# A list schedule that knows TensorE's tilings, and the recurrence's outputs issued in two groups

## The chip, the cores and the metric

The kernel runs on one core of a Trainium2 chip. The metric is device time in microseconds (us) of one execution; the time before is the median of three runs. A core has five engines that run side by side, each through its own list of instructions in order: TensorE (PE in the profile) multiplies matrices, with the loading of the stationary operand shown apart as PEld; VectorE (DVE), ScalarE (ACT) and GpSimd (POOL) work elementwise; SyncE (SP) issues DMAs. An instruction that needs another engine's result waits on a semaphore.

## The reference, cut to what matters

The program is two blocks, one after the other, on 512 tokens of width 1024, all in float32. The first block has two layers (feed-forward, a mixer, feed-forward). The second has two layers, each with three mixers side by side: full attention, neighbourhood attention, and a recurrence with a matrix state for each of six heads, run forwards and backwards, first over a context of 256 tokens and then over the 512 tokens. The change touches the code of this recurrence:

```python
def _rwkv7_step(S, inp):
    r, w, k, v, kk, b = inp
    sa = jnp.einsum('bhvk,bhk->bhv', S, kk)
    S = S * w[:, :, None, :] - sa[..., None] * b[:, :, None, :] + v[..., None] * k[:, :, None, :]
    return S, jnp.einsum('bhvk,bhk->bhv', S, r)
...
    S_f, y_f = lax.scan(_rwkv7_step, S0_f, (r, decay[:, :, 0], kd[:, :, 0], v, kk, bd[:, :, 0]))
    S_b, y_b = lax.scan(_rwkv7_step, S0_b, (r, decay[:, :, 1], kd[:, :, 1], v, kk, bd[:, :, 1]),
                        reverse=True)
```

## The kernel before, in words

**How it is written.** The code does not issue instructions. It records them as `Op` objects, in the order of the program text (with `par` weaving parts that are independent), and `schedule` puts all of them into one order before any is issued; `emit` then issues them, which is why nearly every row of the profile has one line, L568. So a change of the planner's prices can move any instruction of the kernel.

**The planner.** `Op._cost` gives each instruction a price in microseconds. `simulate` is a list scheduler over the five engines: an instruction may start when all that it depends on has ended, plus `lag` (a `LATENCY` by the engine that produced it, nothing from TensorE to TensorE), and when there is a free slot for each new tile. On each engine the ready instruction with the best `key` is taken. `schedule` calls it six times, in turn backwards in time (which gives the keys) and forwards (which gives the order). On TensorE there is one more rule: a ready matmul of the same kind as the last is preferred, if its key is no more than `STAY` = 2.0 us behind the best one. Before the change there are two kinds, `small` (price under 0.1 us) and not small.

**Prices on TensorE.** Before the change, a float32r matmul (one pass over the array) costs 1/2.4 ns a column plus 2 ns, a float32 one four times as much a column, and times 0.58 where its stationary operand has 17 to 64 columns. Large products are made of three float32r matmuls of up to 512 columns (`mm3`); small ones are float32, and the profile shows each float32 matmul as two records.

**Tilings.** A matmul uses a part of the 128 x 128 array: its stationary operand's rows and columns, each rounded up to 32, 64 or 128. This text calls that pair the tiling (128x128, 128x64, 64x64, 64x32, ...), and a place in TensorE's order where the tiling differs from the matmul before a switch. Matmuls of one tiling may stand at different places of the array.

**The recurrence** (`rwkv_d`) takes 32 tokens a step, four steps a block of 128. A step is: six matmuls zeta S of tiling 64x32, two subtractions on VectorE that give the rows of u in the tile `UV`, six matmuls of tiling 64x64 that add to the state, an addition on VectorE that gives the next S. After each fourth step the block's outputs are made: 24 matmuls rho S with the four old states (tiling 64x32, `KR` times `old`), and 12 matmuls Q [u; v] (tiling 128x64, `EQ` times `UV`), into two PSUM tiles `py`, one for each parity of the head. They are recorded as four rho S, two Q [u; v], six times over. There are 20 such blocks in the program (four in the first layer's context, eight in each layer's tokens), so 480 matmuls rho S and 240 Q [u; v]; in the profile rho S and zeta S are `ps<-S,t`, and Q [u; v] is `ps<-uv,t` with 128*64.

Of the kernel before, what the change touches and what calls it, by code (L numbers as in the profile page):

```python
# [12 lines left out]
F32R = mybir.dt.float32r  # L13
# [3 lines left out]
P = 128  # L17
# [246 lines left out]

SLOTS = dict(t=70, raw=4, ps=8, big=3, uv=1, S=14, tmp=2, s8=48, s32=16, s64=4)
ENGINES = ("tensor", "vector", "scalar", "gpsimd", "sync")
LATENCY = dict(tensor=0.2, vector=0.14, scalar=0.15, gpsimd=0.15, sync=3.0)
AHEAD = dict(sync=25.0)
AHEAD_ALL = 80.0
BACK = 500  # L270
# [83 lines left out]
class Op:  # L354
    def __init__(self, eng, method, a, k):
        self.eng, self.method, self.a, self.k = eng, method, a, k
        named = [(f"#{i}", x) for i, x in enumerate(a)] + list(k.items())
        refs = [(q in ("#0", "out", "accum_out"), x) for q, x in named if isinstance(x, Ref)]
        self.writes = [x for w, x in refs if w]
        self.reads = [x for w, x in refs if not w]  # L360
        self.cost = self._cost()
        self.small = self.cost < 0.1 and eng == "tensor"

    def _cost(self):

        n = max([x.cols() for x in self.writes + self.reads] or [1])
        ps = any(x.base.kind == "ps" for x in self.reads)
        if self.eng == "tensor":
            n = self.writes[0].cols()
            if self.method == "transpose":  # L370
                return 0.84e-3 * n
            l = self.k["lhsT"]
            f = 1 / 2.4 if l.base.dt == F32R else 4 / 2.4
            half = 0.58 if 16 < l.cols() <= 64 else 1.0
            return 0.002 + 1e-3 * max(n, 64) * f * half
        if self.eng == "vector":
            if self.method == "reciprocal":
                return 0.065 + 6.25e-3 * n
            fast = not ps and self.method in ("tensor_scalar", "tensor_copy", "memset")
            return 0.07 + n * (0.52e-3 if fast else 1.04e-3) + 0.06 * any(isinstance(self.k.get(q), Ref) for q in ("scalar", "scalar1"))  # L380
        if self.eng == "scalar":
            return (0.051 if ps else 0.094) + 0.833e-3 * n + 0.09 * ("accum_out" in self.k)
        if self.eng == "gpsimd":
            return 0.28 + 0.166 * n if self.k.get("op") == ALU.pow else 0.03 + (0.84e-3 if self.method == "memset" else 2.25e-3) * n
        return 0.05 + 1.65e-3 * n
# [55 lines left out]
def simulate(ops, before, after, key, lag, ahead):  # L441


    n = len(ops)
    left = [len(d) for d in before]
    uses, slot, start = {}, {}, [0.0] * n
    for op in ops:
        for t in op.slotted:
            uses[id(t)] = uses.get(id(t), 0) + 1
    empty = {k: [(0.0, i) for i in range(m)] for k, m in SLOTS.items()}  # L450
    ready, free = [0.0] * n, dict.fromkeys(ENGINES, 0.0)
    wait = {e: [] for e in ENGINES}
    can = {e: [] for e in ENGINES}
    small = False
    first, head, done, order = sorted(range(n), key=key.__getitem__), 0, [False] * n, []
    for i in range(n):
        if not left[i]:
            heapq.heappush(wait[ops[i].eng], (0.0, i))

    def room(i, tight):  # L460

        need = {}
        for t in ops[i].slotted:
            if id(t) not in slot:
                need[t.kind] = need.get(t.kind, 0) + 1
        at = 0.0
        for k, m in need.items():
            if len(empty[k]) - m < (0 if tight or i == first[head] else RESERVE.get(k, 0)):
                return None
            at = max(at, heapq.nsmallest(m, empty[k])[-1][0])  # L470
        return at

    def best(tight):
        out = None
        for e in ENGINES:
            limit = key[first[head]] + ahead(e)
            while wait[e] and wait[e][0][0] <= free[e]:
                i = heapq.heappop(wait[e])[1]
                heapq.heappush(can[e], (key[i], i))
            for src, time in ((can[e], lambda x: free[e]), (wait[e], lambda x: x[0])):  # L480
                pick = None
                for x in sorted(src):
                    i = x[1]
                    if key[i] > limit or pick and key[i] > pick[1] + STAY:
                        if src is can[e]:
                            break
                        continue
                    if pick and ops[i].small != small:
                        continue
                    at = room(i, tight)  # L490
                    if at is not None:
                        pick = (max(at, time(x)), key[i], i, e, src, x)
                        if e != "tensor" or src is not can[e] or ops[i].small == small:
                            break
                if pick:
                    break
            if pick and (out is None or pick[:2] < out[:2]):
                out = pick
        return out

    while len(order) < n:
        while done[first[head]]:
            head += 1
        pick = best(False) or best(True)
        if pick is None:
            return None
        at, _, i, e, src, x = pick
        if e == "tensor":
            small = ops[i].small
        src.remove(x)  # L510
        heapq.heapify(src)
        end = free[e] = at + ops[i].cost
        start[i], done[i] = at, True
        order.append(i)
        for t in ops[i].slotted:
            if id(t) not in slot:
                slot[id(t)] = heapq.heappop(empty[t.kind])[1]
            uses[id(t)] -= 1
            if not uses[id(t)]:
                heapq.heappush(empty[t.kind], (end + 0.1, slot[id(t)]))  # L520
        for j in after[i]:
            ready[j] = max(ready[j], end + lag(i, j))
            left[j] -= 1
            if not left[j]:
                heapq.heappush(wait[ops[j].eng], (ready[j], j))
    return order, slot, [start[i] + ops[i].cost for i in range(n)]


def schedule(ops):

    n = len(ops)
    for op in ops:
        op.slotted = [t for t in op.tiles() if t.kind in SLOTS]
    before = dependences(ops)
    after = [[] for _ in range(n)]
    for i, d in enumerate(before):
        for j in d:
            after[j].append(i)  # L540
    lag = lambda i, j: 0.0 if ops[i].eng == ops[j].eng == "tensor" else LATENCY[ops[i].eng]
    key, far, out = [-float(i) for i in range(n)], BACK, None
    for _ in range(ROUNDS):
        back = simulate(ops, after, before, key, lambda i, j: lag(j, i), lambda e: far)
        ahead = back and simulate(ops, before, after, [-x for x in back[2]], lag, lambda e: AHEAD.get(e, AHEAD_ALL))
        if not ahead:
            break
        out, key, far = ahead, [-x for x in ahead[2]], AGAIN
    return [ops[i] for i in out[0]], out[1]
# [22 lines left out]
class Prog:  # L572
# [47 lines left out]
    def row(self):  # L620
        return self.t2((4, T))
# [1211 lines left out]
    def rwkv_d(self, d, q, r, S):  # L1833


        n, nb, need_y = d["n"], d["nb"], d["need_y"]
        UV = d["UV"]
# [3 lines left out]
        both = [(j, par) for j in range(3) for par in range(2)]  # L1841
        for step in range(4 * nb):
            g = 4 * nb - 1 - step if r else step
            b, c = g // 4, g % 4
            row = lambda c, par: 64 * (c % 2 ^ par)
            if step % 4 == 0:
                old = {}
# [3 lines left out]
            for j, par in both:  # L1851
                o, ro = 64 * par, row(c, par)
# [7 lines left out]
            for j, par in both:  # L1860
                o, ro = 64 * par, row(c, par)
# [3 lines left out]
            self.tt(S, pn, keep, ALU.add)  # L1865
            if not need_y or step % 4 < 3:
                continue
            py = [self.ps((P, 3, 64)) for _ in range(2)]
            for a in range(2):
                for j in range(3):  # L1870
                    for i, par in ((0, 0), (0, 1), (1, 0), (1, 1)):
                        o, cc = 64 * par, 2 * a + (i ^ par)
                        s = P * (b % 2) + 32 * cc
                        self.mm(py[par][32 * cc:32 * cc + 32, j], q["KR"][j][b // 2][o:o + 64, 1, s:s + 32],
                                old[cc][o:o + 64, j], stop=False)
                    for par in range(2):
                        self.mm(py[par][64 * a:64 * a + 64, j], q["EQ"][2 * j + par][:, 2 * b + a], UV[:, b, a, 2 * j + par],
                                start=False)
            for par in range(2):
                y = d["y"][b][:, par::2]  # L1880
                if first:
# [207 lines left out]
```

## Time and profile before

| | |
|---|---|
| time before, median of three runs | 3327.55 us (3325.96 to 3327.77) |
| the profiled execution: its own time | 3327.22 us |
| its span, first to last instruction | 3325.4 us |
| TensorE busy | 3217.1 us (97% of the span), 21142 records |
| VectorE, ScalarE, GpSimd busy | 2299.8 us (69%), 1613.3 us (49%), 252.0 us (8%) |
| mean granted TensorE clock | 0.987 |

The first two rows are times of the device, and the rest is read from one profiled execution. A busy share is an average over stages; a busy TensorE is not one at its peak, since the end of a matmul is modelled and matmuls overlap. So the start-to-start distance between rows says more than a row's own duration. [...]

### The profile page before, as it was taken

Reading aid. Unit: us, or ns where it says so; the run is one execution under the profiler, and the core shown is the slowest. Engines: PE = TensorE matmul, PEld = TensorE weight load, DVE = VectorE, ACT = ScalarE, POOL = GpSimd, SP = SyncE. Lnnn points to the kernel's source line nnn. Section 1 sums busy time; section 2 is a strip of 40 time slices with the busy share of each in tenths; the row PEclk is TensorE's granted clock in tenths of the full one; section 3 lists DMA queues with packets and bytes.
Section 4 is the critical chain, followed back from the end, with each engine's and each line's share of the span. In section 5 each row is a group of like instructions: output and inputs, shape, how many; then the busy total and the mean of one; then the engine's idle time right before and its main releaser. Section 6 shows DMA issues by size and latency. Waiting matters only on the chain. (4 is left out here: it accounts for less than half of the span.)

```text
span 3325.4 us, 55255 instructions
## 1 busy us (share of the span) xinstructions
PE 3217.1 (97%) x21142; PEld 2604.3 (78%) x21142; DVE 2299.8 (69%) x4801; ACT 1613.3 (49%) x3579; POOL 252.0 (8%) x233
## 2 busy tenths in 40 slices
PE   8999999999999999999999999999999898999898
PEld 6788878778877788878886888777877678877677
DVE  9954686575669677677568657587475887575876
ACT  4433464363434344333338535344454974654773
POOL 0000000000000102000001000000120011111111
PEclk9999999999999999999999999999999999999899
DMA  6633332133213334344431422233222232322231
GB/s 227 205 114 124 120 116 80 56 117 101 82 55 101 108 117 143 114 137 154 130 103 38 133 88 89 69 102 120 89 83 93 66 118 94 107 87 85 63 121 43
DMA packets 153489, 348.41 MB, mean 105 GB/s; under 512 B 16644, under 2 KB 60420, under 8 KB 153224
## 3 DMA queue, kind: packets, MB, share of 16 engines
q1 hardware_dynamic: 153224, 344.87, 31.9%
q8 instruction: 166, 2.72, 0.3%
q14 instruction: 99, 0.81, 0.1%
HBM read 315.05 MB, written 29.76 MB: 104 GB/s over the span
## 5 line engine op out<-in xcount | busy, mean ns | idle before, releaser
L568 PE MATMUL ps<-t,t 128*128 128x512 f32 (+6 forms) x15204 | 2865.1, 351 | 63.7 <-DVE t L568 29.6
L568 PEld LDWEIGHTS ps<-t,t 128*128 128x128 f32 (+2 forms) x15204 | 2287.6, 182 | 522.6 <-issue 65.2
L568 ACT ACTIVATE t<-raw 128x512 fp32r<-128x512 f32 (+1 forms) x962 | 565.8, 612 | 762.5 <-PE ps L568 510.5
L568 DVE TENSOR_TENSOR t<-raw,t 128x512 fp32r<-128x512 f32 (+2 forms) x962 | 625.5, 670 | 235.3 <-PE ps L568 169.0
L568 ACT ACTIVATE t<-t 128x512 f32<-128x512 f32 (+8 forms) x739 | 377.7, 525 | 426.4 <-DVE t L568 246.2
L568 DVE TENSOR_TENSOR t<-t,t 128x256 f32<-128x256 f32 (+7 forms) x812 | 417.7, 544 | 91.3 <-ACT t L568 57.1
L568 ACT ACTIVATE t<-ps 128x512 f32<-128x512 f32 (+8 forms) x448 | 216.0, 511 | 219.5 <-PE ps L568 214.6
L568 DVE TENSOR_TENSOR t<-ps,t 128x512 f32<-128x512 f32 (+3 forms) x274 | 178.8, 657 | 185.3 <-PE ps L568 178.2
L568 POOL TENSOR_TENSOR s<-s,const 128x4 f32<-128x4 f32 (+6 forms) x65 | 110.2, 1698 | 1722.4 <-DVE s L568 1714.0
L568 PE MATMUL ps<-const,t 128*128 128x128 f32 (+1 forms) x1116 | 189.0, 291 | 22.5 <-ACT t L568 12.3
L568 DVE SCALAR_TENSOR_TENSOR t<-ps,t 128x512 f32<-128x512 f32 (+3 forms) x229 | 147.5, 648 | 69.2 <-PE ps L568 68.5
L568 PEld LDWEIGHTS ps<-const,t 128*128 128x128 f32 x1116 | 137.4, 149 | 66.1 <-ACT t L568 27.8
L568 PE MATMUL ps<-uv,t 64*64 64x64 f32 (+1 forms) x2208 | 144.1, 230 | 3.2 <-DVE t L568 1.7
L568 PEld LDWEIGHTS ps<-uv,t 64*64 64x64 f32 (+1 forms) x2208 | 103.5, 135 | 52.9 <-issue 14.1
L568 ACT ACTIVATE t<-t,const 128x256 f32<-128x256 f32 (+3 forms) x165 | 102.0, 646 | 52.4 <-DVE t L568 30.5
L568 ACT ACTIVATE uv<-ps 32x128 f32<-32x128 f32 (+1 forms) x288 | 92.5, 322 | 59.4 <-PE ps L568 55.4
L568 DVE SCALAR_TENSOR_TENSOR t<-t,t 128x512 f32<-128x512 f32 (+2 forms) x116 | 76.7, 663 | 64.0 <-ACT t L568 62.6
L568 DVE SCALAR_TENSOR_TENSOR t<-raw,const,t 128x512 f32<-128x512 f32 x168 | 117.9, 744 | 1.4 <-DMA raw<-in_wmod_dram 1.4
L568 DVE TENSOR_TENSOR uv<-uv,ps 32x192 f32<-32x192 f32 x192 | 66.5, 347 | 65.7 <-PE ps L568 58.1
L568 POOL TENSOR_TENSOR S<-S,s 128x192 f32<-128x192 f32 x96 | 62.2, 648 | 599.5 <-DVE S L568 451.0
L568 PE MATMUL ps<-S,t 64*32 64x64 f32 x2112 | 104.0, 224 | 0.6 <-DVE S L568 0.6
L568 ACT ACTIVATE t<-ps,s,s 128x256 f32<-128x256 f32 (+1 forms) x140 | 88.1, 650 | 26.4 <-DVE s L568 26.3
(81 smaller groups left out, 1388.0 us busy)
## 6 DMA issues: line engine op xcount, KB each, us to landing
raw<-in_wgu_dram SPq DMA_DIRECT2D x176, 512.0 KB, 3.6
raw<-in_win_dram SPq DMA_DIRECT2D x88, 512.0 KB, 3.6
raw<-in_wd_dram SPq DMA_DIRECT2D x128, 256.0 KB, 2.7
raw<-in_wmod_dram SPq DMA_DIRECT2D x48, 512.0 KB, 3.8
t<-dram SPq DMA_DIRECT2D x68, 256.0 KB, 2.8
dram<-t SPq DMA_DIRECT2D x68, 256.0 KB, 2.0
t<-dram SPq DMA_DIRECT2D x97, 128.0 KB, 2.2
raw<-in_wd_dram SPq DMA_DIRECT2D x64, 192.0 KB, 2.3
```

The lines of the kernel that those rows point to most:

```text
L568: getattr(getattr(tc.nc, op.eng), op.method)(*map(real, op.a), **{q: real(v) for q, v in op.k.items()})
```

## The change: what it does

Five edits. The planner's `LATENCY` of TensorE goes from 0.2 to 0.22 and that of VectorE from 0.14 to 0.13, and whatever TensorE waits for from another engine is planned 0.12 us later (`INTO_PE`). Each matmul's tiling is recorded, and the preference for the same kind becomes one for the same tiling. A switch costs the planner 0.12 us (`RETILE`). Matmuls get new prices, those of small float32 ones divided by how many of them the tiling takes side by side (`SIDE_BY_SIDE`). In `rwkv_d` a block's outputs are recorded as all rho S, then all Q [u; v]; for that only the first head pair's rho S carries `start`.

```diff
--- before.py
+++ after.py
@@ -264,7 +264,12 @@
 
 SLOTS = dict(t=70, raw=4, ps=8, big=3, uv=1, S=14, tmp=2, s8=48, s32=16, s64=4)
 ENGINES = ("tensor", "vector", "scalar", "gpsimd", "sync")
-LATENCY = dict(tensor=0.2, vector=0.14, scalar=0.15, gpsimd=0.15, sync=3.0)
+LATENCY = dict(tensor=0.22, vector=0.13, scalar=0.15, gpsimd=0.15, sync=3.0)
+INTO_PE = 0.12
+
+SIDE_BY_SIDE = {(128, 128): 1, (128, 64): 2, (128, 32): 4, (64, 128): 2, (64, 64): 4, (64, 32): 6, (32, 128): 4,
+                (32, 64): 6, (32, 32): 8}
+RETILE = 0.12
 AHEAD = dict(sync=25.0)
 AHEAD_ALL = 80.0
 BACK = 500
@@ -358,8 +363,14 @@
         refs = [(q in ("#0", "out", "accum_out"), x) for q, x in named if isinstance(x, Ref)]
         self.writes = [x for w, x in refs if w]
         self.reads = [x for w, x in refs if not w]
+        self.tiling = self._tiling() if eng == "tensor" else None
         self.cost = self._cost()
-        self.small = self.cost < 0.1 and eng == "tensor"
+
+    def _tiling(self):
+
+        l = self.reads[0] if self.method == "transpose" else self.k["lhsT"]
+        up = lambda n: 32 if n <= 32 else 64 if n <= 64 else 128
+        return up(32 * l.v.shape[0]), up(l.cols())
 
     def _cost(self):
 
@@ -368,11 +379,11 @@
         if self.eng == "tensor":
             n = self.writes[0].cols()
             if self.method == "transpose":
-                return 0.84e-3 * n
-            l = self.k["lhsT"]
-            f = 1 / 2.4 if l.base.dt == F32R else 4 / 2.4
-            half = 0.58 if 16 < l.cols() <= 64 else 1.0
-            return 0.002 + 1e-3 * max(n, 64) * f * half
+                return 0.003 + 0.833e-3 * n
+            if self.k["lhsT"].base.dt == F32R:
+                return 0.0137 + n / 2400
+            one = max(0.003 + n / 1200, 0.11 if self.tiling[1] == P else 0.08)
+            return 2 * max(one / SIDE_BY_SIDE[self.tiling], 0.02)
         if self.eng == "vector":
             if self.method == "reciprocal":
                 return 0.065 + 6.25e-3 * n
@@ -451,7 +462,7 @@
     ready, free = [0.0] * n, dict.fromkeys(ENGINES, 0.0)
     wait = {e: [] for e in ENGINES}
     can = {e: [] for e in ENGINES}
-    small = False
+    tiling = None
     first, head, done, order = sorted(range(n), key=key.__getitem__), 0, [False] * n, []
     for i in range(n):
         if not left[i]:
@@ -485,12 +496,13 @@
                         if src is can[e]:
                             break
                         continue
-                    if pick and ops[i].small != small:
+                    same = ops[i].tiling == tiling
+                    if pick and not same:
                         continue
                     at = room(i, tight)
                     if at is not None:
                         pick = (max(at, time(x)), key[i], i, e, src, x)
-                        if e != "tensor" or src is not can[e] or ops[i].small == small:
+                        if e != "tensor" or src is not can[e] or same:
                             break
                 if pick:
                     break
@@ -505,8 +517,8 @@
         if pick is None:
             return None
         at, _, i, e, src, x = pick
-        if e == "tensor":
-            small = ops[i].small
+        if e == "tensor" and ops[i].tiling != tiling:
+            at, tiling = at + RETILE, ops[i].tiling
         src.remove(x)
         heapq.heapify(src)
         end = free[e] = at + ops[i].cost
@@ -538,7 +550,10 @@
     for i, d in enumerate(before):
         for j in d:
             after[j].append(i)
-    lag = lambda i, j: 0.0 if ops[i].eng == ops[j].eng == "tensor" else LATENCY[ops[i].eng]
+    def lag(i, j):
+        pe = ops[j].eng == "tensor"
+        return 0.0 if pe and ops[i].eng == "tensor" else LATENCY[ops[i].eng] + INTO_PE * pe
+
     key, far, out = [-float(i) for i in range(n)], BACK, None
     for _ in range(ROUNDS):
         back = simulate(ops, after, before, key, lambda i, j: lag(j, i), lambda e: far)
@@ -1865,6 +1880,7 @@
             self.tt(S, pn, keep, ALU.add)
             if not need_y or step % 4 < 3:
                 continue
+
             py = [self.ps((P, 3, 64)) for _ in range(2)]
             for a in range(2):
                 for j in range(3):
@@ -1872,10 +1888,11 @@
                         o, cc = 64 * par, 2 * a + (i ^ par)
                         s = P * (b % 2) + 32 * cc
                         self.mm(py[par][32 * cc:32 * cc + 32, j], q["KR"][j][b // 2][o:o + 64, 1, s:s + 32],
-                                old[cc][o:o + 64, j], stop=False)
-                    for par in range(2):
-                        self.mm(py[par][64 * a:64 * a + 64, j], q["EQ"][2 * j + par][:, 2 * b + a], UV[:, b, a, 2 * j + par],
-                                start=False)
+                                old[cc][o:o + 64, j], start=(j == 0), stop=False, skip_group_check=True)
+            for a in range(2):
+                for j, par in both:
+                    self.mm(py[par][64 * a:64 * a + 64, j], q["EQ"][2 * j + par][:, 2 * b + a], UV[:, b, a, 2 * j + par],
+                            start=False, skip_group_check=True)
             for par in range(2):
                 y = d["y"][b][:, par::2]
                 if first:
```

No instruction is added or taken away: both programs have 17,144 matmuls (12,016 of them float32r), 1,041 DMAs, 3,300 activations, and the same elementwise work. What changes is the order. Counted over the whole of TensorE's order, there are 1,392 switches before and 950 now. The rho S stand in 198 runs of their tiling before and in 53 now, the Q [u; v] in 184 and in 50. Switches between 64x32 and 128x64 go from 326 to 54, those between 128x64 and 128x128 from 400 to 295.

Three places on TensorE show it. The first is the fourth block of the second layer's forward pass over the tokens, where the names are a PSUM tile, a state or `uv`, and the stationary tile. Before:

```order
L568 MATMUL ps_31656<-S_30447,t_28452 32x64
L568 MATMUL ps_31656<-S_30623,t_28452 32x64
L568 MATMUL ps_31656<-uv_27908,t_29094 64x64
L568 MATMUL ps_31656<-S_30447,t_28470 32x64
L568 MATMUL ps_31656<-S_30623,t_28470 32x64
L568 MATMUL ps_31656<-uv_27908,t_29187 64x64
L568 MATMUL ps_31656<-S_30447,t_28477 32x64
L568 MATMUL ps_31656<-S_30623,t_28477 32x64
L568 MATMUL ps_31656<-uv_27908,t_29650 64x64
```

Two rho S, then one Q [u; v], and so on: the tiling switches twice in three matmuls. Of the same block now, these are the end of its rho S and the start of its Q [u; v]:

```order
L583 MATMUL ps_31062<-S_30650,t_28445 32x64
L583 MATMUL ps_31062<-S_30612,t_28445 32x64
L583 MATMUL ps_31062<-S_30650,t_28461 32x64
L583 MATMUL ps_31062<-S_30612,t_28461 32x64
L583 MATMUL ps_31062<-S_30650,t_28469 32x64
L583 MATMUL ps_31062<-S_30612,t_28469 32x64
L583 MATMUL ps_31016<-uv_27928,t_29011 64x64
L583 MATMUL ps_31016<-uv_27928,t_29141 64x64
L583 MATMUL ps_31016<-uv_27928,t_29645 64x64
L583 MATMUL ps_31016<-uv_27928,t_29011 64x64
L583 MATMUL ps_31016<-uv_27928,t_29141 64x64
L583 MATMUL ps_31016<-uv_27928,t_29645 64x64
```

Eighteen rho S of this block stand in a row there, with one switch to the Q [u; v] behind them. The second place is in the first block's feed-forward, into which the context's attention is woven (a product with the values, PSUM tile ps_3575 before, four matmuls of tiling 128x64). Before:

```order
L568 MATMUL ps_3575<-t_3550,t_3287 64x128
L568 MATMUL ps_3554<-t_3533,t_3447 128x512
L568 MATMUL ps_3575<-t_3550,t_3287 64x128
L568 MATMUL ps_3554<-t_3548,t_3423 128x512
L568 MATMUL ps_3575<-t_3550,t_3287 64x128
L568 MATMUL ps_3554<-t_3533,t_3423 128x512
L568 MATMUL ps_3575<-t_3550,t_3287 64x128
L568 MATMUL ps_1624<-t_3526,t_901 128x512
```

Each of the four stands alone between two matmuls of 512 columns. The same product now:

```order
L583 MATMUL ps_3598<-t_3446,t_3485 128x512
L583 MATMUL ps_3608<-t_3569,t_3370 64x128 x4
L583 MATMUL ps_3618<-const_212,t_3584 128x128 x4
L583 MATMUL ps_3598<-t_3468,t_3434 128x512
L583 MATMUL ps_3598<-t_3446,t_3434 128x512
```

The four have moved together, with two switches where there were eight.

## Rows read from the trace of the kernel before

**Rows 1.** The page's busy time of each engine, share of span, instructions.

```profile
PE 3217.1 (97%) x21142; PEld 2604.3 (78%) x21142; DVE 2299.8 (69%) x4801; ACT 1613.3 (49%) x3579; POOL 252.0 (8%) x233
```

**Rows 2.** Windows: length, each engine's busy us (instructions), granted clock, DMA share, GB/s.

```profile
0.00:600.00 600.00, 583.28 (x2870) 481.85 (x2871) 418.09 (x769) 263.75 (x521) 16.03 (x18) 1.00 0.42 139
...
1800.00:2400.00 600.00, 595.21 (x3411) 473.26 (x3412) 401.08 (x758) 285.77 (x634) 38.32 (x34) 0.99 0.29 96
2400.00:3325.40 925.40, 859.54 (x8289) 689.20 (x8288) 661.56 (x1568) 542.61 (x1274) 119.65 (x120) 0.96 0.27 87
```

**Rows 3.** Waits on TensorE: for whom, us in total, times, longest.

```profile
PE ps L568 <- DVE t L568: 44.6, 24, 15.6
PE ps L568 <- ACT t L568: 39.0, 41, 4.0
PE ps L568 <- ACT big L568: 6.3, 6, 1.9
PE ps L568 <- POOL s L568: 5.1, 5, 2.3
```

**Rows 4.** Timeline of TensorE: start, us, form, records; the alternation's ends.

```profile
3145.67 0.30 PE L568 MATMUL ps<-S,t 64*32 64x64 f32 x4
3145.90 0.33 PE L568 MATMUL ps<-uv,t 128*64 128x64 f32 x2
3146.16 0.30 PE L568 MATMUL ps<-S,t 64*32 64x64 f32 x4
...
3150.32 0.33 PE L568 MATMUL ps<-uv,t 128*64 128x64 f32 x2
3150.58 0.67 PE L568 MATMUL ps<-const,t 128*128 128x128 f32 x2
```

**Rows 5.** Timeline of TensorE in the first layer's context recurrence.

```profile
988.34 0.33 PE L568 MATMUL ps<-uv,t 128*64 128x64 f32 x2
988.59 0.30 PE L568 MATMUL ps<-S,t 64*32 64x64 f32 x4
...
990.58 0.32 PE L568 MATMUL ps<-S,t 64*32 64x64 f32 x8
990.82 0.45 PE L568 MATMUL ps<-uv,t 128*64 128x64 f32 x4
991.20 0.53 PE L568 MATMUL ps<-S,t 64*32 64x64 f32 x14
991.65 1.45 PE L568 MATMUL ps<-t,t 128*128 128x512 f32 x5
993.03 0.56 PE L568 MATMUL ps<-uv,t 64*64 64x64 f32 x12
...
996.47 0.53 PE L568 MATMUL ps<-S,t 64*32 64x64 f32 x18
996.93 1.20 PE L568 MATMUL ps<-t,t 128*128 128x512 f32 x4
998.05 0.33 PE L568 MATMUL ps<-uv,t 128*64 128x64 f32 x2
```

**Rows 6.** Timeline of TensorE: one tiling without a switch.

```profile
1046.24 20.72 PE L568 MATMUL ps<-t,t 128*128 128x512 f32 x90
1066.79 0.27 PE L568 MATMUL ps<-const,t 128*128 128x128 f32 x1
```

**Rows 7.** Timeline of TensorE at the second place; forms merged by name.

```profile
382.77 4.25 PE L568 MATMUL ps<-t,t 128*128 128x512 f32 x16
386.87 0.60 PE L568 MATMUL ps<-const,t 128*128 128x128 f32 x4
```

**Rows 8.** Timeline of TensorE: four matmuls of tiling 128x64 in one run.

```profile
686.92 0.66 PE L568 MATMUL ps<-t,t 128*64 128x128 f32 x8
687.50 0.66 PE L568 MATMUL ps<-const,t 128*128 128x128 f32 x4
```

**Rows 9.** Groups of VectorE: the recurrence's two elementwise steps.

```profile
L568 DVE TENSOR_TENSOR uv<-uv,ps 32x192 f32<-32x192 f32 x192 | 66.5, 347 | 65.7 <-PE ps L568 58.1 <-ACT uv L568 4.9
L568 DVE TENSOR_TENSOR S<-ps,S 128x192 f32<-128x192 f32 x96 | 34.1, 356 | 49.7 <-PE ps L568 48.8
```

**Rows 10.** Windows: the stretch in which VectorE is busiest, and one after alternation.

```profile
3150.60:3157.50 6.90, 6.90 (x37) 5.60 (x36) 3.24 (x7) 4.54 (x12) 0.00 (x0) 0.51 0.24 76
2600.00:2700.00 100.00, 88.60 (x928) 71.25 (x928) 86.96 (x222) 85.11 (x215) 6.97 (x8) 0.95 0.28 83
```

## The prediction, made before the changed kernel ran

> **What bounds the kernel now.** I read the busy shares first: TensorE is busy for 97% of the span, VectorE for 69%, ScalarE for 49% [rows 1]. Such a share could still hide stages with another limit, so the windows come next: TensorE is busy 583 of the first 600 us, 595 of the 600 us up to 2400, and 860 of the last 925 [rows 2]. The last stretch, in which the second block runs, is the loosest, and even there TensorE idles for only 7%. Then the waits: of the gaps of over 150 ns on TensorE the four largest causes come to 95 us over the program [rows 3]; all are of the kind "wait for a VectorE, ScalarE or GpSimd result", none for a DMA. So TensorE is the bound nearly everywhere, and time taken out of its own list should leave the total, as long as the waits do not grow by as much.
>
> TensorE being busy doesn't mean that it multiplies. In the timeline, at the place where the order had two rho S and one Q [u; v] in turn, the row of rho S starts 0.23 us before the Q [u; v], and that 0.26 us before the next rho S [rows 4]. The ten pairs from 3145.67 to 3150.58 take 4.91 us for 30 matmuls of 64 columns, 0.16 us each, while 90 matmuls of 512 columns in one tiling take 20.55 us, 0.228 each [rows 6]. There is no wait in those pairs; the time is in the switches. What does a switch cost? Between two rows of small tilings, four and five matmuls of 512 columns take 1.12 and 1.38 us from start to start [rows 5]. Without switches they would take 0.91 and 1.14. So going in and out costs 0.21 to 0.24, and one switch 0.11.
>
> **The change, part by part.** The number of instructions of every kind stays, so only order can change the time. Matmuls first, priced by start-to-start distances.
>
> *Q [u; v].* A run of one matmul (two records) lasts 0.26 us [rows 4], of two 0.38 [rows 5]. So one more matmul costs 0.12, and 0.14 us is the run's own, paid once. 184 runs become 50: 134 × 0.14 = 18.8 us less. The 240 × 0.12 us stay: these matmuls use all rows of the array and the same columns, and grouping does not overlap them.
>
> *rho S.* A run of two lasts 0.23 us [rows 4], of four 0.24, of seven 0.45, of nine 0.46 [rows 5]. With the same fixed 0.14 a matmul costs (0.45 - 0.14)/7 = 0.044 or (0.46 - 0.14)/9 = 0.036. Before: 198 runs with 2.4 matmuls on average, 198 × 0.235 = 46.5 us. After: 53 × 0.14 + 480 × 0.044 = 28.5 us. That is 18.0 less. No run of 18 or 24 exists in the trace, so I bound it: with 0.036 it is 21.8 less; with the 0.058 that a matmul of the row with tiling 64x64 costs ((0.49 - 0.14)/6, 993.03 to 993.52 [rows 5]) it is 11.3 less. I take 18, because rho S itself gives the nearest rows.
>
> *All other switches.* 442 switches go away, and a run's length above, from its start to the next one's, holds the switch at its end: 145 and 134. There remain 163. The low price is 0.11: 18 us. The high price comes from the second place in the order: 16 records, of which eight are matmuls of 512 columns, take 4.10 us from 382.77 to 386.87 [rows 7]. Less 8 × 0.228 that is 2.28 us for four matmuls that stand alone. Four in one run take 0.58 [rows 8], 0.69 with the way in. So 1.59 us for six switches, 0.26 each, and 163 of those would be 43 us. Only where single matmuls of one product are brought together is so much to be had; most of the 163 are single switches beside matmuls of 128 columns and more. I take 0.16, nearer the low end: 26 us.
>
> *Waits.* Fewer switches also mean less TensorE work behind which the other engines hide. The recurrence has 96 steps with two handoffs each; the one for u needs two VectorE operations of 0.35 us, the one for S one of 0.36 [rows 9], and the semaphores. Counted in the two orders with the prices above, 5 of these 192 handoffs had less than 0.9 us of TensorE work between them, and 18 now. Thirteen times at most 0.4 us makes 5; I take 2. All other waits [rows 3] I leave as they are: they stand where a norm or a softmax is awaited, and the change gives these no shorter path. The new latencies change nothing by themselves, since they are not in the program; they move instructions, which costs nothing while TensorE has other matmuls ready, and up to the whole gap where it has none. DMAs: the same 1,041, and TensorE's waits name none.
>
> *Sum.* 18.8 + 18.0 + 26 - 2 = 61 us. The profiled execution took 3327.2 us, 0.3 below the median of the runs, so 3327.2 - 61 = **3266 us**. With the low ends (18.8 + 11.3 + 18 - 5) it is 3284, with the high ones (18.8 + 21.8 + 43) 3244.
>
> [...]
>
> **Rivals.**
>
> *The waits shrink too.* The planner's new prices are closer to the start-to-start rows than the old ones (it had 0.064 us for a Q [u; v] that takes 0.12, and nothing for a switch), so its order should meet results more nearly when they are ready. For it: TensorE has 95 us of such gaps, and 66 us of its 108 idle us lie in the last 925 [rows 1, 2]. Against it: the largest gaps are at norms, where nothing else is ready. If a third goes, the time is 3266 - 33 = 3233.
>
> *The gain is taken by waits.* From 2600 to 2700 us VectorE is busy for 87 us and ScalarE for 85, TensorE for 89 [rows 10]: there a shorter TensorE list runs into the other two engines. For it: such stretches lie where the recurrence and the attention of the second block are, and there most of the switches were. Against it: over the last 925 us VectorE is busy for 662, so it has room on average. If half is lost, 3266 + 30 = 3296.
>
> *Slower.* The preference for the same tiling may hold a step of the recurrence back by up to 2.0 us behind matmuls whose key is worse. The 96 steps are one chain per direction, and if each comes later by d while TensorE has nothing else, 96 × d is added; it decides from d = 61/96 = 0.64 us. At 1 us the time is 3266 + 96 = 3362. Against it: TensorE has other work in nearly every gap of the recurrence (VectorE's two steps are awaited by TensorE in none of the large groups of [rows 3]).
>
> [...]
>
> [...]
>
> **How the numbers follow.** The likeliest case, 3245 to 3285, has 0.62. Shrinking waits, 3215 to 3245, have 0.17: the prices are better, but gaps at norms stay. Waits that take much of it, 3285 to 3320, have 0.14. Slower has 0.04, nothing changed 0.03. The range 3220 to 3305 holds the first case and most of the second and third, and leaves out some 0.15. A change of 0.2% (6.7 us) is about the least that a measurement of this kernel can tell from none; by it the first three cases are faster (0.93), and the others are 0.03 and 0.04.
>
> **What would show it.** In the changed profile rho S should stand in rows of up to 48 records with some 0.02 us a record, and Q [u; v] in rows of up to 24 with 0.06; no stretch should alternate like [rows 4]; at the second place eight records should take 0.6 us in one row. TensorE's gaps should sum to about 95 us again, VectorE's and ScalarE's busy times should be the same to a per cent, and their shares of the span higher. If the gaps are above 130 us, the second rival is right; if they are under 70, the first. If long rows of rho S cost 0.1 us a matmul, my price for them was wrong.

## The result and the profile after

The changed kernel takes 3274.07 us, median of four runs (3273.36 to 3274.92), against 3327.66 for the kernel before beside it: a ratio of 0.9839, 95% interval 0.9822 to 0.9857. That is 53.6 us less where the prediction said 61, and inside its range. The profiled span is 3271.7 us, 53.7 less than before.

The page's busy times and three windows answer to [rows 1, 2]:

```profile
PE 3155.5 (96%) x21142; PEld 2585.5 (79%) x21142; DVE 2308.9 (71%) x4801; ACT 1605.7 (49%) x3579; POOL 254.1 (8%) x233
```

```profile
0.00:600.00 600.00, 583.42 (x2895) 485.39 (x2896) 418.50 (x765) 264.92 (x523) 14.92 (x18) 1.00 0.44 140
...
1800.00:2350.00 550.00, 548.16 (x3171) 442.78 (x3168) 372.38 (x704) 253.29 (x553) 39.34 (x33) 1.00 0.32 102
2350.00:3271.70 921.70, 847.68 (x8355) 692.71 (x8353) 675.27 (x1573) 550.59 (x1292) 116.66 (x120) 0.95 0.28 88
```

The work is the same (21142 records, and the other engines' busy times to 1%), and TensorE is busy for 61.6 us less. So the time came out of TensorE's own list. Where in it, the timeline of the third block of the second layer's forward pass shows (start, us, form, records):

```profile
3036.51 1.21 PE L583 MATMUL ps<-S,t 64*32 64x64 f32 x60
3037.65 1.08 PE L583 MATMUL ps<-uv,t 128*64 128x64 f32 x24
3038.66 0.73 PE L583 MATMUL ps<-t,t 128*128 128x512 f32 x2
3039.33 0.82 PE L583 MATMUL ps<-S,t 64*32 64x64 f32 x36
3040.08 0.73 PE L583 MATMUL ps<-uv,t 128*64 128x64 f32 x14
3043.00 0.86 PE L583 MATMUL ps<-t,t 64*64 64x64 f32 x11 [2.19 <-ACT t L583]
```

All 12 Q [u; v] of a block now start within 1.01 us, and 30 rho S (six of them the next block's) within 1.14. In [rows 4] ten Q [u; v] and twenty rho S took 4.91 us. Two things are to be seen besides. A Q [u; v] in this row costs (1.01 - 0.14)/12 = 0.073 us, not the 0.12 that [rows 5] gave for the second of two. This row is the exception: of the five rows of twelve at the full clock (a granted clock of 1) and without a wait, the other four take 1.36 us, 0.102 a matmul. One of them:

```profile
1077.65 1.43 PE L583 MATMUL ps<-uv,t 128*64 128x64 f32 x24
1079.01 0.49 PE L583 MATMUL ps<-t,t 128*128 128x512 f32 x1
```

By the program's places in the array, the first six matmuls there use one half of its columns and the next six the other, and most starts are 0.117 us apart. In the row at 3037.65 the half changes after every three, and nearly all starts are 0.058 us apart. And behind the rows TensorE waits for 2.19 us for a ScalarE result.

At the second place four matmuls that stood alone in [rows 7] stand together and take 0.59 us to the next row's start:

```profile
389.51 0.66 PE L583 MATMUL ps<-t,t 128*64 128x128 f32 x8
390.10 0.33 PE L583 MATMUL ps<-const,t 128*128 128x128 f32 x1
```

TensorE's gaps by what ended them, to be read beside [rows 3]:

```profile
PE ps L583 <- DVE t L583: 57.6, 29, 15.6
PE ps L583 <- ACT t L583: 31.6, 48, 2.2
PE ps L583 <- DVE s L583: 4.4, 1, 4.4
PE ps L583 <- DVE uv L583: 3.5, 9, 1.4
...
PE ps L583 <- DVE S L583: 2.3, 5, 0.9
```

The recurrence's two handoffs are the waits for `uv` and `S`. Before, they were:

```profile
PE ps L568 <- DVE uv L568: 1.1, 3, 0.5
...
PE ps L568 <- DVE S L568: 0.6, 2, 0.3
```

All rows of this view sum to 106.4 us in 103 gaps; before, to 98.2 in 85. Waits for ScalarE's `t` fell from 39.0 to 31.6 us, and those for VectorE's `t` rose from 44.6 to 57.6. The gain in the list is a little larger than the gain in time, and the gaps hold 8 us of the difference.

The mean granted clock, before, after, and in a second execution of the changed kernel (e8):

```profile
core 0: 3325.4 us, clock 0.987
```

```profile
core 0: 3271.7 us, clock 0.982
```

```profile
core 0: 3269.3 us, clock 0.981
```

The clock's record has two levels and no other, 1 and 0.5, before as after. So a mean of 0.987 is 2 × 0.013 × 3325 = 86 us at the lower one, and 0.982 is 118. At 0.5 a float32r matmul of 512 columns inside a row starts 0.43 us before the next one, against 0.23 at 1 (medians of before, 26 starts and 8581). From these two numbers I estimate that a stretch at the lower level costs up to about half of itself while TensorE has work.

To add up the whole, I took the start-to-start distance of every TensorE record in both traces (a wait counts to the record before it) and summed by kind, in us. The columns of waits hold the gaps over 150 ns that are inside these sums:

| kind | before | after | difference | waits in it, before | after | difference without waits |
|---|---|---|---|---|---|---|
| rho S | 47.8 | 25.3 | -22.5 | 0.8 | 0.7 | -22.3 |
| Q [u; v] | 53.6 | 33.5 | -20.1 | 0.0 | 2.5 | -22.6 |
| other float32 of tilings 128x64 (128 and 193 columns), 128x32, 64x128, 64x64, 128x128 | 380.7 | 353.5 | -27.2 | 35.4 | 27.5 | -19.2 |
| float32r products | 2590.5 | 2594.0 | +3.5 | 27.8 | 35.7 | -4.4 |
| transposes | 160.1 | 165.9 | +5.8 | 16.2 | 22.2 | -0.2 |
| zeta S, the products E [u; v] and tiling 32x128 | 69.1 | 75.8 | +6.7 | 2.4 | 2.1 | +7.1 |

### The profile page after: what moved, and what is told of

Its sections match the earlier page's. It is cut to its first block, busy times and chain, and to the rows that moved or that the text cites. A ratio compares the mean times of both kernels' runs of the same rounds, so it can differ in the third digit from the quotient of the medians.

```text
span 3271.7 us, 55264 instructions
## 1 busy us (share of the span) xinstructions
PE 3155.5 (96%) x21142; PEld 2585.5 (79%) x21142; DVE 2308.9 (71%) x4801; ACT 1605.7 (49%) x3579; POOL 254.1 (8%) x233
## 5 line engine op out<-in xcount | busy, mean ns | idle before, releaser
L583 ACT ACTIVATE t<-t 128x512 f32<-128x512 f32 (+9 forms) x739 | 375.5, 525 | 377.7 <-DVE t L583 241.0
L583 PE MATMUL ps<-const,t 128*128 128x128 f32 x1116 | 191.1, 289 | 30.3 <-DVE t L583 14.4
L583 PEld LDWEIGHTS ps<-const,t 128*128 128x128 f32 x1116 | 133.7, 147 | 75.8 <-ACT t L583 31.0
L583 PEld LDWEIGHTS ps<-uv,t 128*64 128x64 f32 (+1 forms) x2208 | 94.7, 138 | 45.6 <-issue 19.1
L583 PE MATMUL ps<-uv,t 128*64 128x64 f32 (+1 forms) x2208 | 120.1, 231 | 4.1 <-DVE uv L583 3.5
L583 ACT ACTIVATE t<-ps,const 128x256 f32<-128x256 f32 (+1 forms) x100 | 56.8, 577 | 81.1 <-PE ps L583 80.7
```

The source lines that it names most:

```text
L583: getattr(getattr(tc.nc, op.eng), op.method)(*map(real, op.a), **{q: real(v) for q, v in op.k.items()})
```

## The experiments

Theory 1 is the prediction's: a switch costs about 0.12 us of TensorE's time (53.6 us for 442, a price taken from the result), and the time follows the number of switches. Theory 2: the better prices and latencies shorten TensorE's waits, and switches are a side matter. Times are medians; "less" and "more" are against the kernel before on the same chip, unless another is named.

**Each half of the change alone.** e1 has all edits of the planner and the old recording:

```diff
-                                old[cc][o:o + 64, j], start=(j == 0), stop=False, skip_group_check=True)
-            for a in range(2):
-                for j, par in both:
-                    self.mm(...)
+                                old[cc][o:o + 64, j], stop=False)
+                    for par in range(2):
+                        self.mm(...)
```

> All edits of the planner, but the block outputs recorded as before (four rho S, two Q [u; v], six times over). Its order has 1,189 switches, 203 fewer than before; rho S stands in 185 runs (198 before, 53 in the change), Q [u; v] in 166. Theory 1, that switches are the cost at about 0.12 us each (53.6 us for 442): 203 x 0.12 = 24 us less than before, about 3303. Theory 2, that the better prices and latencies shorten TensorE's waits and the switches are a side matter: most of the gain is here already, 3275 to 3285, with TensorE's gaps well below the 95 us of before.

3298.18 us, 27 less than 3325.33 (ratio 0.9911, interval 0.9895 to 0.9928). e2 is the kernel before with the new recording, the same lines the other way:

> Only the recorded order of the block outputs changes, the planner is that of before. 1,157 switches, 235 fewer than before; rho S in 67 runs, Q [u; v] in 48. Theory 1: 235 x 0.12 = 28 us less than before, about 3299, and the two tilings 64x32 and 128x64 lose some 37 us of start-to-start time. Theory 2: within 10 us of before, 3318 to 3328.

3300.28 us, 25 less (0.9921, 0.9906 to 0.9936). Both came out as theory 1 said, and each half brings about half. In e2 rho S and Q [u; v] fell from 101.4 to 60.1 us, and in e1 they stayed at 102.8. So of 41 us that these two lost in e2, 25 reached the total: TensorE's gaps rose from 98.2 to 107.6 us there. The 0.12 us is what a switch less brings net of such losses, and not the price of the switch alone.

**Parts of the planner.** e3 takes the prices and latencies back, and leaves the tilings and the new recording:

```diff
-LATENCY = dict(tensor=0.22, vector=0.13, ...
-INTO_PE = 0.12
+LATENCY = dict(tensor=0.2, vector=0.14, ...
+INTO_PE = 0.0
...
-            one = max(0.003 + n / 1200, 0.11 if self.tiling[1] == P else 0.08)
-            return 2 * max(one / SIDE_BY_SIDE[self.tiling], 0.02)
...
+            return 0.002 + 1e-3 * max(n, 64) * f * half
```

> The changed kernel with the old prices of matmuls and the old latencies: what is new in the planner is only that it prefers the same tiling and pays 0.12 us for a switch. 925 switches, 467 fewer than before. Theory 1: 467 x 0.12 = 56 us less than before, about 3271, no worse than the changed kernel. Theory 2: the waits come back, 3295 to 3310.

3267.37 us, 58 less (0.9822, 0.9808 to 0.9837). e4 keeps the new prices, and takes back the preference and the price of a switch (`_old` gives the price of before):

```diff
-RETILE = 0.12
+RETILE = 0.0
...
         self.cost = self._cost()
+        self.tiling = eng == "tensor" and self._old() < 0.1
...
```

> The changed kernel with the new prices and latencies, but with the two kinds of matmul of before and no price for a switch. 1,165 switches, 227 fewer than before, nearly all from the new order of the block outputs. Theory 1: 227 x 0.12 = 27 us less than before, about 3300. Theory 2: as fast as the changed kernel, 3270 to 3280.

3311.68 us, only 14 less (0.9965, 0.9954 to 0.9975). e7 takes back the latencies alone:

```diff
-LATENCY = dict(tensor=0.22, vector=0.13, ...
-INTO_PE = 0.12
+LATENCY = dict(tensor=0.2, vector=0.14, ...
+INTO_PE = 0.0
```

> The changed kernel with the latencies of before (TensorE 0.2, VectorE 0.14, nothing added for what TensorE waits for). 927 switches, 23 fewer than in the changed kernel. Theory 1: 3 us less by the switches, so 3265 to 3275, and the new latencies are worth nothing that can be told. Theory 2: more waits on TensorE, 3285 or more.

3268.08 us, 57 less (0.9829, 0.9815 to 0.9844). Theory 2 has fallen: without the new prices and latencies the gain is all there. e4 still has the new recording, which brought 25 us by itself in e2; with the new prices and latencies added to it the kernel is 11 us slower than e2. e4 also missed theory 1, by 12 us. Its gaps are not larger (96.7 us), but its mean clock is 0.976, some 159 us at the lower level, and in e2, which has nearly the same number of switches, 0.985 or 99 us. (The 0.976 is of the profiled run, which took 3319.7 us; six of the eight runs of e4 had 0.978 to 0.980.)

**More switches.** e5 takes the changed kernel's schedule and pulls runs of a small tiling apart before it is issued:

```diff
     ops, slot = schedule(ops)
+    ops = apart(ops)
...
+        if ops[pe[j]].tiling != full and k - j >= 2 and k < len(pe) and ops[pe[k]].tiling == full:
...
+                if x is None or ops[x].tiling != full or new[x] or any(to.get(d, d) > pe[i] for d in before[x]):
+                    break
+                to[x] = pe[i]
```

> The changed kernel's schedule, in which afterwards each run of a small tiling that is followed by matmuls of tiling 128x128 is taken apart: one small matmul, one of 128x128, and so on, where the order of results allows it. Prices, order on all other engines and all work stay; 1,815 switches, 865 more than in the changed kernel. Theory 1: 865 x 0.11 to 0.12 = 95 to 104 us more than the changed kernel, 3369 to 3378. A rival, that a switch costs nothing where a large matmul stands beside it and the gain came from the packing of small ones alone: not over 3300.

3486.38 us, 213 more than the changed kernel on the same chip (e8, 3273.49), twice what was expected. The rival that had switches free beside large matmuls is out, but a switch put in is dearer here than a switch taken out. It is not waits: TensorE's gaps sum to 89.1 us. The groups of the changed kernel and of e5 show where (form, count, busy us and mean ns, idle before):

```profile
L583 PE MATMUL ps<-t,t 128*128 128x512 f32 x9120 | 2256.6, 397 | 29.2 <-DVE t L583 20.1 <-ACT t L583 4.6 <-DVE s L583 4.4
...
L583 PE MATMUL ps<-t,t 64*64 64x64 f32 x960 | 31.3, 243 | 8.7 <-ACT t L583 4.0 <-DVE t L583 3.2 <-ACT big L583 1.4
```

```profile
L616 PE MATMUL ps<-t,t 128*128 128x512 f32 x9120 | 2383.5, 404 | 24.4 <-DVE t L616 18.2 <-ACT t L616 6.1
...
L616 PE MATMUL ps<-t,t 64*64 64x64 f32 x960 | 70.5, 269 | 8.5 <-DVE t L616 4.9 <-ACT t L616 3.6
```

The large products' busy time rose by 127 us, and that of these 960 small records from 31.3 to 70.5 us. The small ones had shared the array (31.3 us of busy time for 960 × 243 ns); now 102 of their 480 matmuls stand alone in their tiling, and others in shorter runs. But the mean clock is 0.963 there (some 258 us at the lower level), so e11 does the same in the first half alone, where before and after the lower level hardly appears (some 20 us in each):

```diff
-    while j < len(pe):
+    while j < 8800:
```

> The changed kernel's schedule with runs of small tilings taken apart in its first half alone (the first 8,800 matmuls), where TensorE has the fewest gaps. 1,254 switches, 304 more than in the changed kernel. At 0.12 a switch 36 us more, about 3310. At the 0.25 of the run that took apart the whole program (213 us for 865) 76 us more, about 3350. The difference between the two is what small matmuls lose beside the switch, by no longer standing next to each other, and what the lower clock level adds: if it is the clock, the first half, which spends little time at the lower level, should come near 0.12.

3336.5 us (ratio 1.0037, 1.0025 to 1.0048). The changed kernel's ratio gives 3271.8 beside this run's 3325.33 for the kernel before, so 65 us more for 304 switches: 0.21 each, nearer the 0.25 of e5 than 0.12, with a mean clock of 0.981, as in e8, and with gaps of 96.7 us against 106.4. So the extra is neither mainly the clock nor waits. By start-to-start distances without waits, the large products take 27 us more and the small tilings 43. A tiling that ran at the full clock in both, in the changed kernel and in e11:

```profile
L583 PE MATMUL ps<-t,const 128*32 128x128 f32 x308 | 17.4, 285 | 3.4 <-ACT t L583 3.4
```

```profile
L616 PE MATMUL ps<-t,const 128*32 128x128 f32 x308 | 27.1, 285 | 2.9 <-ACT t L616 2.9
```

A record lasts 285 ns in both, and the same 308 take longer together: they overlap less. So one switch more costs the switch and also the small matmul's company. The price of the switch itself stands in the trace of before (medians at the full clock, without waits). A float32r matmul of 512 columns starts 0.23 us before the next one inside a row, 0.34 as the first after a switch, 0.32 as the last before one, and 0.43 alone: 0.20 for the two switches of a lone one, 0.10 each. A run of small matmuls pays on its own side too: its last rho S starts 0.146 us before whatever comes next, where rho S inside the row of 30 are 0.03 apart. The sum of both sides, and the company, is why 0.21 and 0.25 are nearer the 0.26 that the prediction read from [rows 7] and [rows 8] than its 0.11.

**Fewer switches.** e9 and e10 start from e3 and let the preference reach further:

```diff
-STAY = 2.0
+STAY = 4.0
```

and in e10

```diff
-STAY = 2.0
+STAY = 8.0
```

> The kernel of the run with the old prices and latencies (3267), in which a matmul of the same tiling is now preferred up to 4.0 us behind the best key instead of 2.0. 835 switches, 90 fewer than there. If a switch goes on costing 0.12 us and waits stay, 11 us less: about 3256. If holding others back now costs waits, as the prediction's slower rival has it: 3267 or more.

> The same with 8.0 us. 754 switches, 171 fewer than the run with the old prices and latencies. By the switches alone 171 x 0.12 = 21 us less: about 3247. If the holding back costs waits, less gain than with 4.0 us, or none: 3256 to 3275, with TensorE's gaps above the 106 us of the changed kernel.

3284.42 us (0.9877, 0.9863 to 0.9892) and 3269.15 (0.9831, 0.9816 to 0.9846): 17 more than e3 for 90 switches fewer, and about the same as e3 for 171 fewer. TensorE's gaps tell why. In e9 they sum to 142.0 us, in e10 to 131.0, in e3 to 109.4: 33 and 22 us more waits against 11 and 21 us that the switches were to save. The first rows of e9:

```profile
PE ps L583 <- DVE t L583: 51.2, 31, 16.7
PE ps L583 <- ACT t L583: 41.0, 52, 3.0
PE ps L583 <- ACT big L583: 16.9, 11, 3.5
PE ps L583 <- DVE uv L583: 10.5, 14, 2.6
PE ps L583 <- DVE S L583: 7.5, 12, 1.2
```

The recurrence's two handoffs, `uv` and `S`, cost 18.0 us here, 8.7 in e3 and 9.3 in e10. The mechanism of the prediction's slower rival, holding steps of the chain back, can so be 9 of e9's 33 us; the others are waits for other results, and in e10, where the preference reaches twice as far, the handoffs cost hardly more than in e3. Why the shorter reach of e9 is the slower one stays open.

**Columns in turn.** e6 is the changed kernel with the outputs recorded so that neighbours use other columns of the array:

```diff
-            for a in range(2):
-                for j in range(3):
+            for j in range(3):
+                for a in range(2):
...
-            for a in range(2):
-                for j, par in both:
+            for j, par in both:
+                for a in range(2):
```

> The changed kernel with the block outputs recorded so that neighbours use different columns of the array: rho S over all four column groups before the next head pair, Q [u; v] with the two column halves in turn. 959 switches, 9 more than in the changed kernel. If Q [u; v] cost 0.12 us each because neighbours use the same columns, as the prediction has it, they should fall to some 0.06 (a run of eight that alternate takes 0.62 us in the trace of before) and rho S to some 0.03: 240 x 0.06 + 480 x 0.015 = 22 us less than the changed kernel, about 3252. If the 0.12 is a cost of each matmul whatever its place: no change, 3270 to 3278.

3277.42 us, 4 more than the changed kernel beside it (0.9857 and 0.9845, intervals that overlap). Q [u; v] fell from 33.5 to 25.3 us and rho S from 25.3 to 23.7, less than half of what was expected, and the total kept none of it. TensorE's gaps sum to 116.9 us, 10.5 more than in the changed kernel, which is as much as the two kinds lost; the waits for VectorE's `t` alone rose from 57.6 to 70.5. The mean clock is 0.978, some 144 us at the lower level. e12 does the same on e3:

> The run with the old prices and latencies (3267), with the outputs recorded over the columns in turn. 934 switches, 9 more. With the changed planner that order of columns took 12 us out of the tiling 128x64 and gave nothing in the total, while the time at the lower clock level rose from 122 to 144 us. If the loss was a chance of that schedule, 10 us less than the base here: about 3257. If what TensorE saves there turns into waits and a lower clock again: 3265 to 3272.

3265.36 us (0.9817, 0.9800 to 0.9834), 2 less than e3, with a spread of 14 us between its runs: no difference that can be told. It has the lowest median of all, but stands within the intervals of e3 and e7.

**The changed kernel once more.**

> The changed kernel once more, for its trace. If the stretches at the lower clock level are set by the order of the instructions, they stand at the same places for about the same 122 us; if they are a chance of the execution, their sum differs by tens of us and the time with it by up to half of that.

3273.49 us, and the lower clock at the same places. Two windows of the changed kernel, then of e8 (us, busy times, clock, DMA):

```profile
2572.50:2581.60 9.10, 9.10 (x111) 8.19 (x110) 6.59 (x17) 8.85 (x26) 2.70 (x3) 0.50 0.00 1
3117.60:3135.70 18.10, 16.98 (x72) 14.91 (x74) 12.62 (x28) 6.07 (x18) 0.00 (x0) 0.50 0.15 46
```

```profile
2572.50:2581.60 9.10, 8.44 (x87) 7.12 (x82) 6.57 (x15) 8.88 (x26) 3.45 (x3) 0.50 0.00 1
3117.60:3135.70 18.10, 18.03 (x85) 15.94 (x85) 10.64 (x26) 8.58 (x25) 0.00 (x0) 0.50 0.18 52
```

By the clock's own record some 83 us at the lower level fall on the same time in both executions. So the lower level belongs to the order, in its larger part, and is not a chance of one execution.

Time by switches, for all variants with fewer switches than before:

| | switches less than before | us less | us a switch |
|---|---|---|---|
| changed kernel | 442 | 53.6 | 0.12 |
| e1 planner only | 203 | 27.2 | 0.13 |
| e2 order only | 235 | 25.1 | 0.11 |
| e3 tilings only | 467 | 58.0 | 0.12 |
| e4 prices only | 227 | 13.7 | 0.06 |
| e6 columns | 433 | 47.3 | 0.11 |
| e7 old latencies | 465 | 56.6 | 0.12 |
| e9, e10 longer preference | 557, 638 | 40.9, 56.2 | 0.07, 0.09 |
| e12 tilings, columns | 458 | 60.0 | 0.13 |

## Why the prediction was right, step by step

**That TensorE's own list is the bound** held: 61.6 us fewer of busy time became 53.6 us of time.

**Q [u; v]:** 18.8 us predicted, 20.1 measured (22.6 without waits). The number is right, and the sentence behind it, that grouping overlaps none of them, holds only where several in turn use the same columns: there most matmuls of a long row cost 0.117 us, close to the 0.12. Near a change of the half they cost 0.058, and with the halves in turn in e6 a row of twelve takes 0.93 us instead of 1.36. So e6's idea was right for these matmuls. It had less to gain than I expected because the changed kernel's rows hold such changes already, and most are short (240 matmuls in 50 rows).

**rho S:** 18.0 predicted, 22.5 measured. In the row of 30 a matmul costs (1.14 - 0.14)/30 = 0.033, just under the bound 0.036 from a run of nine; the 0.044 that I took was from a run of seven.

**All other switches:** 26 us predicted, at 0.16 each. The other small tilings lost 27.2, but 7.9 of these are waits that stand at other kinds now; without waits they lost 19.2, the float32r products 4.4, and the transposes 0.2, while the last row of the table took 7.1 more. Net that is 16.7 us. This is the term that was mis-sized, by 9 us, together with the waits. What took the 9 is not shown: a part can be the lower clock.

**The sum of the list** was 62.8 us, and TensorE's busy time fell by 61.6. That is so near partly by luck: rho S and Q [u; v] gave 8 us more than their terms, and the other switches 9 less.

**Waits:** 2 us predicted. The gaps grew by 8.2, and these 6 us make most of the 7 by which 61 was too much. Half of the growth, 4.1, is at the recurrence's two handoffs (1.7 to 5.8 us), for which the prediction had 5 us at most; the other half is at the waits that it left as they were.

**The clock:** The sum has no term for it, though [rows 10] show 6.9 us at 0.51 behind the alternation. There are some 32 us more at the lower level (86 to 118), worth up to 16, and these are inside the list's terms. It is argued from sums, not isolated: no run here changes the clock and nothing else. But e8 shows that its places come in the larger part with the order, and e4, which missed by its switches without larger gaps, had more of it.

**The rivals.** The waits did not shrink, and the gain does not need the new prices and latencies (e3, e7). The second rival, a gain taken by waits, came true for 8 us of gaps and not for 30; the mark of 130 us that the prediction set for it was not reached in the changed kernel, only in e9 and e10, where the preference reaches further.

**The price of a switch.** Most runs that only merge neighbours give 0.11 to 0.13 net (the changed kernel, e1, e2, e3, e6, e7, e12; e4 gives 0.06, and e9 and e10 0.07 and 0.09); those that isolate small matmuls give 0.21 and 0.25 (e11, e5). So a change of the tiling costs time, and how much depends on what stands on both sides. What it is at a switch that takes the time is not shown: no run here separates one cause from another at the same place.

## What to carry to other kernels

Where TensorE mixes tilings and is the bound, count the places where the tiling changes in its order, and read the price of one from the start-to-start distance of short rows between long ones; here that gave the size of the gain to an eighth, with errors of 8 and 9 us that cancelled. A scheduler needs little to use it: beside the new recording, a preference for the same tiling and a price for a change did as much as with refitted prices and latencies (which of the two does it was not separated). How far the preference should reach is not settled: 2, 4 and 8 us behind the best key gave 58, 41 and 56 us, one order each, and the longer reaches made TensorE wait for 33 and 22 us more.

## What the runs showed of the hardware that was not expected

Float32 matmuls of tiling 128x64 with 64 columns mostly start 0.117 us apart where six in turn use the same half of the array's columns, and 0.058 where the half changes every three: the same twelve take 1.36 or 1.01 us. Taking runs of tiling 128x32 apart, at the full clock, raised the busy time of the same 308 records from 17.4 to 27.1 us. A lone 512-column product between two switches starts 0.43 us before the next matmul, against 0.23 in a row. And a shorter TensorE list had more of the lower clock, not less: 118 us against 86, at places that in the larger part repeat from one execution to the next.
